# Sparse attention: where the bias tile is loaded, how the mask is made, and the order of the splits and fills

## The chip, the cores and the metric

One core of one Trainium2 chip runs the whole program in one launch. TensorE multiplies matrices; VectorE, ScalarE and GpSimd work on tiles in on-chip memory (SBUF, and PSUM for matmul results); SyncE, and here also ScalarE and GpSimd, issue the DMAs. The metric is the device time of one execution in microseconds, as the median of several executions. The profile is one further execution, recorded by the hardware profiler.

## The reference, cut to what matters

A two-layer model with 256 tokens of 1024 features: a recurrent layer with an MLP, a sparse attention layer with an MLP, and a closing block. The change concerns the sparse attention: an indexer scores all keys of a query, the 64 best causal keys are kept, and softmax runs over these with a bias that depends on the distance and the head.

```python
q, c, qi, ki, wi = jnp.split(h @ w_in, ATT_IN_SPLITS, axis=-1)
...
dots = jax.nn.relu(jnp.einsum('bqhd,bsd->bqhs', qi_b, ki))          # 8 index heads
score = jnp.einsum('bqh,bqhs->bqs', wi_b, dots)
score = jnp.where(causal[None], score, -jnp.inf)
_, idx = lax.top_k(score, topk)                                     # topk = 64
...
bias = jnp.moveaxis(rel_bias[t5_bucket(dist)], -1, 2)               # by distance, 16 heads
logits = jnp.einsum('bqhc,bqkc->bqhk', q_lat_b, c_sel) + bias
logits = jnp.where((dist >= 0)[:, :, None, :], logits, -jnp.inf)
p = jax.nn.softmax(logits, axis=-1)
return jnp.einsum('bqhk,bqkc->bqhc', p, c_sel)
```

The kernel doesn't gather. It computes the logits of all keys and adds a very large negative number (NEG, -1e30) to those that are not among the 64 or lie in the future.

## The kernel before, in words

**Products.** Every float32 product is made of three matmuls of a faster 32-bit type, on the high and the low part of both operands (mm3, L235 to L239). Each weight chunk of 128 x 1024 numbers (512 KB) therefore takes three steps (wt_part, L222 to L225): SyncE's queue loads it into w_raw, ScalarE copies it to w_hi, and VectorE subtracts and gets w_lo. There are four buffers for w_raw and six each for w_hi and w_lo. While K.pool is set, GpSimd does the subtraction instead (pooled), and that split is put behind the last score instruction issued so far (K.scored).

**Order.** Most instructions go to a tile scheduler, which orders them for each engine by priorities. Where K.pin is set, or keep_in_program_order is called, the instruction stands in the order of the source. An order written out by hand interleaves the parts of the attention: run(s0, n) advances the scores of query block 0 by n steps, and pooled(next_q), q_half(i), k_part(j) and v_part(h) are put between. After it, a list of fills gives TensorE something to do between a turn and the product that follows it.

**Stages.** rec_layer; mlp(0), in 16 groups, each with an up and a down product, into which hook0 mixes other work: ada_raw loads on SyncE's queue with dot products on VectorE, and, in group 2, t5_bias_rows, which computes 16 rows (one per head) of 384 bias numbers by distance and writes them to DRAM by GpSimd's queue (t5_rows); att_layer; mlp(1); the closing block.

**The attention.** cki is the projection that holds the latent, the index key and the head weights. qi_ps are the four index-query projections (two pairs), from chunks 2 to 5 of w_att_in. tz is a tile of 128 x 16 x 256 numbers: for each query row and head the bias row, shifted by one number from row to row. It is read from t5_rows in four DMAs of 512 KB with rows of 1 KB; they stand on ScalarE's queue behind the low part of the last weight chunk (load_tz, L704 to L712). scores(t) makes the score of query block t: eight heads on TensorE, ScalarE and VectorE, and then eight rounds of MAX and MATCH_REPLACE on VectorE, each of which finds the eight largest numbers and replaces them by TAKEN. The mask follows (L833 to L840): dg is the larger of "not taken" and noncausal on the diagonal 128 x 128 square, and msk is dg times NEG; block 1 also has a first square without a diagonal. q_half(0..7) are the query projections (two make one q_ps and one qT); k_part makes the keys and v_part the values. soft adds bias and mask (l_mb, L877), makes the logits (l_ps, L886), adds both with a running maximum (l_s, L893; l_nm is its negative), and ScalarE takes exponentials (L899). turn transposes the result (pT_ps, copied to pT by VectorE or ScalarE in turn, L915 and L917), weigh multiplies by the values (o_ps, L927), and o_sb divides by the sum.

Of the kernel before, what the change touches and what calls it, by code (L numbers as in the profile page):

```python
# [10 lines left out]
F32 = mybir.dt.float32  # L11
# [3 lines left out]
ALU = mybir.AluOpType  # L15
# [5 lines left out]
P = 128  # L21
S = 256
# [11 lines left out]
NEG = -1e30  # L34
LOWEST = -3e38
TAKEN = -3.4e38
TAKEN_CUT = -3.2e38
IDX_W_SCALE = 8 ** -0.5 * 64 ** -0.5
NBKT, MAXD = 32, 128
TZW = 384  # L40
# [119 lines left out]
def _tile_stack(ctx, tc, ins, out):  # L160
    nc = tc.nc
    K = _Ctx()
# [3 lines left out]
    pin = tc.keep_in_program_order  # L166
    const = ctx.enter_context(tc.tile_pool(name="const", bufs=1))
# [7 lines left out]
    def behind(later, earlier):  # L175
        tc.add_manual_dep(later.ins, earlier.ins.name,
                          mybir.DependencyInfo(mybir.DependencyClass.Sync, mybir.DependencyReason.DATA),
                          reason="load order")
# [51 lines left out]
    def wt(src, k):  # L230
        raw, hi, lo = wt_tiles()
        wt_part(raw, hi, lo, src, slice(0, CH))
        return [h.rearrange("p (k c) -> p k c", k=k) for h in (hi, lo)]
# [443 lines left out]
    def att_layer():  # L677
        with tc.tile_pool(name="att", bufs=1) as a1, tc.tile_pool(name="att2", bufs=2) as a2:
            att_body(a1, a2)

    def att_body(a1, a2):
# [15 lines left out]

        xT = transposed(xt, "mix1", (0, 1), lambda: c.append(wt(ins["w_att_in"][1], 4)), cki_rows, cki_rows)
        wq = [wt(ins["w_att_in"][2 + i], KT) for i in range(2)]
        K.pin = False  # L700
        rs = [rms_stat(xt[t], "r") for t in range(2)]
        b = cki[0]
        tz_after = wt.last
        tz = a1.tile([P, 16, S], F32, name="tz")  # L704

        def load_tz(after):
            for q in range(4):
                behind(nc.scalar.dma_start(tz[:, 4 * q:4 * q + 4],
                                           bass.AP(tensor=K.t5_rows.tensor, offset=K.t5_rows.offset + 1 + 4 * q * TZW,
                                                   ap=[[1, P], [TZW, 4], [1, S]])), after)  # L710

        load_tz(tz_after)  # L712

        noncausal = K.noncausal
        low = a1.tile([P, S], F32, name="low")
        nc.vector.memset(low[:, :P], 0.0)
# [65 lines left out]
        def k_part(j):  # L782
            b = ps("k_ps")
            for i in range(2):
                col = (2 * j + i) * P
                mm3(b[:, i * S:(i + 1) * S], [h[:, 0, col:col + P] for h in uk], (cTh, cTl), True, True)
            k = a1.tile([P, 2, S], F32, name=f"kT{j}")
            nc.scalar.activation(k.rearrange("p a b -> p (a b)"), b, AF.Copy)
            kT.extend([k[:, 0], k[:, 1]])
# [15 lines left out]
        def scores(t):  # L805
            nk = P * (t + 1)
            sc = [a1.tile([P, nk], F32, name=f"score{t}_{i}") for i in range(2)]
            prev = low[:, S - nk:]
            hb = 512 // nk
            parts = []  # L810
            for g in range(8 // hb):
                b = ps("sc_ps")
                par, base = g % 2, (g // 2) * 2 * hb
                hl = [base + par + 2 * j for j in range(hb)]
                o = par * 64
                for j, h in enumerate(hl):
                    nc.tensor.matmul(b[:, j * nk:(j + 1) * nk], qiT[h // 2][o:o + 64, t * P:(t + 1) * P],
                                     kiT[o:o + 64, :nk], start=True, stop=True)
                r = a2.tile([P, 512], F32, name="sc_r")
                rl = nc.scalar.activation(r, b, AF.Relu)  # L820
                for j, h in enumerate(hl):
                    m = pin(nc.vector.scalar_tensor_tensor(sc[0], r[:, j * nk:(j + 1) * nk], wis[t][:, h:h + 1], prev,
                                                       op0=ALU.mult, op1=ALU.add))
                    prev = sc[0]
                    K.scored = m
                yield
            for rd in range(8):
                mx = a2.tile([P, 8], F32, name="top8")
                pin(nc.vector.max(out=mx, in_=sc[rd % 2]))
                pin(nc.vector.match_replace(out=sc[(rd + 1) % 2], in_to_replace=mx, in_values=sc[rd % 2],  # L830
                                            imm_value=TAKEN))
                yield
            m = a1.tile([P, nk], F32, name=f"msk{t}")  # L833
            if t:
                pin(nc.vector.tensor_scalar(m[:, :P], sc[0][:, :P], TAKEN_CUT, NEG, op0=ALU.is_gt, op1=ALU.mult))
            dg = a2.tile([P, P], F32, name="dg")
            pin(nc.vector.scalar_tensor_tensor(dg, sc[0][:, nk - P:], TAKEN_CUT, noncausal,
                                               op0=ALU.is_gt, op1=ALU.max))
            pin(nc.vector.tensor_scalar(m[:, nk - P:], dg, NEG, None, op0=ALU.mult))
            msk.append(m)  # L840

        qT = []
# [1 line left out]
        def q_half(i):  # L844
            if i == len(qw):
                next_q()
            if i % 2 == 0:
                q_half.b = ps("q_ps", "acc")
            b = q_half.b
            j = i % 2  # L850
            prod_a(b[:, j * S:(j + 1) * S], qw[i], xT)
            if j:
                q = a1.tile([P, 2, S], F32, name=f"qT{i // 2}")
                m = nc.vector.scalar_tensor_tensor(q, b.rearrange("p (j s) -> p j s", j=2), 0.125, rB2,
                                                   op0=ALU.mult, op1=ALU.mult)
                if K.pin:
                    pin(m)
                qT.extend([q[:, 0], q[:, 1]])
# [114 lines left out]
        def run(steps, n=1):  # L973
            for _ in range(n):
                next(steps, None)
# [7 lines left out]
        def soft_pair(m):  # L983
            gr, it = items[m]
            return [(gr, it + i, *sh) for i, sh in enumerate(soft(gr, it))]

        def pooled(f):
            K.pool = True
            f()
            behind(wt.last, K.scored)  # L990
            K.pool = False

        uv = []
        s0, s1 = scores(0), scores(1)
        run(s0, 2)
        next_q()
        run(s1, 2)
        q_half(0)
        run(s1, 2)
        q_half(1)  # L1000
        pooled(lambda: uv.extend(wt(ins["w_att_ukv"][1], 1)))
        run(s0, 5)
        pooled(next_q)
        q_half(2)
        run(s0, 4)
        v_part(0)
        q_half(3)
        pooled(next_q)
        pend = soft_pair(0)
        run(s1, 4)  # L1010
        k_part(2)
        q_half(4)
        pooled(next_q)
        run(s1, 5)
        K.pin = False
        fills = [units(), units((q_half, 5)), units((k_part, 3)), units((q_half, 6)), units((q_half, 7)),
                 units((v_part, 1)), units()]
# [3 lines left out]
        for m in range(6):  # L1021
# [7 lines left out]
            pend = cur  # L1029
# [7 lines left out]
    def t5_bias_rows(const):  # L1037
        rb = const.tile([NBKT, 16], F32, name="rel_bias")
        nc.gpsimd.dma_start(rb, ins["rel_bias"])
        oh = const.tile([NBKT, TZW], F32, name="onehot")  # L1040
        nc.gpsimd.dma_start(oh, ins["onehot"])
        b = ps("t5_ps")
        nc.tensor.matmul(b[:16, :TZW], rb, oh, start=True, stop=True)
        r = const.tile([16, TZW], F32, name="t5_sb")
        nc.vector.tensor_copy(r, b[:16, :TZW])
        rows = dram.tile([16, TZW], F32, name="t5_rows")
        nc.gpsimd.dma_start(rows, r)
        return rows
# [4 lines left out]
    def ada_start():  # L1053
        cond = vec("cond", 0, 16)
        th = sm.tile([P, 16], F32, name="silu_t", bufs=1)
        behind(nc.scalar.activation(th, cond, AF.Tanh, scale=0.5), wt.last)
        nc.vector.scalar_tensor_tensor(th, th, 1.0, cond, op0=ALU.add, op1=ALU.mult)
        nc.vector.tensor_scalar(th, th, 0.5, None, op0=ALU.mult)
        ada.update(sc=th, ad=const.tile([P, 16, 2], F32, name="ada"))
# [546 lines left out]
                nc.sync.dma_start(out[0, t * P:(t + 1) * P, sl], f)  # L1606

    rec_layer()
    with tc.tile_pool(name="mlp0", bufs=2) as mp:
        ada_start()  # L1610

        def hook0(g):
            if g == 0:
                K.steps = ada_steps(mp)
            if g == 2:
                K.t5_rows = t5_bias_rows(mp)
                K.noncausal = const.tile([P, P], F32, name="noncausal")
                behind(nc.gpsimd.dma_start(K.noncausal, ins["noncausal"]), K.last)
            next(K.steps, None)
            if g in (7, 12):  # L1620
                next(K.steps, None)
        mlp(0, lambda name, dt: mp.tile([P, 2 * S], dt, name=name), hook0)
    att_layer()
    with tc.tile_pool(name="blk", bufs=1) as b1, tc.tile_pool(name="blk2", bufs=2) as b2:
        early = []

# [32 lines left out]
```

## Time and profile before

| what | value |
|---|---|
| time, median of 3 runs | 896.39 us (893.65 to 897.42) |
| profiled execution | 895.19 us, its span 893.4 us |
| TensorE matmuls (PE) | 876.2 us busy, 98%, 5502 instructions |
| VectorE (DVE) | 684.7 us, 77%, 1191 |
| ScalarE (ACT) | 464.2 us, 52%, 744 |
| GpSimd (POOL) | 51.4 us, 6%, 62 |
| DMA | 162.81 MB, 182 GB/s in the mean |

The span is the time from the first recorded instruction to the last. A share of the span is a mean over stages: the attention is a small part of it, from about 270 to 390 us, and its gaps are seen on the timeline of the engine that sets the end, not in the table. A timeline row has a start and a duration; rows of TensorE overlap, since matmuls are pipelined, so the pitch from start to start counts and not the duration. In brackets stands the idle time before the row and the instruction whose end released it. Names ending in q (ACTq, SPq) are the engine's DMA issues.

### The profile page before, as it was taken

What the parts mean: (1) busy time and instruction counts of PE and PEld (TensorE: products, weight loads), DVE (VectorE), ACT (ScalarE), POOL (GpSimd) and SP (SyncE); (2) the same over time, 40 slices, a digit from 0 to 9 for tenths busy, and PEclk for the clock granted to TensorE, in tenths of its full rate; (3) what the DMA queues carried; (4) which work ended last, traced back from release to release, by engine and by line L of the source; (5) the groups of instructions that cost most, each with busy time, mean ns of one, the idle gap of its engine ahead of it and who ended that gap; (6) DMA issues with size and microseconds to landing.
All of it is one profiled execution on the core that took longest, in us unless ns stands there. A gap on an engine that the chain in (4) does not pass through costs nothing.

```text
span 893.4 us, 14243 instructions
## 1 busy us (share of the span) xinstructions
PE 876.2 (98%) x5502; PEld 777.8 (87%) x5502; DVE 684.7 (77%) x1191; ACT 464.2 (52%) x744; POOL 51.4 (6%) x62
## 2 busy tenths in 40 slices
PE   9999999999999989999999999999999999999998
PEld 7998888888888877888788888898899999989997
DVE  6979789999665898587687777777779987557665
ACT  6895654444455556465465444464445444445441
POOL 3400100000001120000000000111010000000000
PEclk9999999999999999999999999999999999999999
DMA  6646678886653631327976666345253444434541
GB/s 260 209 147 209 230 244 289 285 285 216 212 188 94 213 129 61 143 91 254 289 234 221 231 253 221 118 163 168 95 187 101 162 142 139 145 118 165 182 150 48
DMA packets 47575, 162.81 MB, mean 182 GB/s; under 512 B 5217, under 2 KB 8561, under 8 KB 47506
## 3 DMA queue, kind: packets, MB, share of 16 engines
q1 hardware_dynamic: 44690, 158.39, 52.2%
q10 hardware_dynamic: 2400, 2.31, 0.9%
q0 software_dynamic: 416, 1.19, 0.4%
q8 instruction: 43, 0.70, 0.3%
q14 instruction: 26, 0.21, 0.1%
HBM read 160.80 MB, written 1.07 MB: 181 GB/s over the span
## 4 chain that ended last, share of the span: by engine, by line
PE 71%; issue 17%; DVE 6%; DMA 3%; ACT 1%; POOL 1%; ACTq 0%; SPq 0%; POOLq 0%; DVEq 0%
PE up_ps L249 12%; PE acc_ps L239 7%; PE acc_ps L237 7%; PE acc_ps L238 7%; PE up_ps L252 6%; PE acc_ps L280 2%; PE z_ps L239 2%; PE z_ps L238 2%; PE z_ps L237 2%; PE pj_ps L239 2%; PE pj_ps L237 2%; PE pj_ps L238 2%; DVE w_lo L225 1%; DMA nb<-in_rpb_dram 1%; PE mg_ps L239 1%
## 5 line engine op out<-in xcount | busy, mean ns | idle before, releaser
L224 ACT ACTIVATE w_hi<-w_raw 128x1024 fp32r<-128x1024 f32 (+1 forms) x269 | 278.0, 1054 | 210.2 <-PE z_ps L238 63.8
L225 DVE TENSOR_TENSOR w_lo<-w_raw,w_hi 128x1024 fp32r<-128x1024 f32 (+1 forms) x265 | 318.0, 1215 | 86.7 <-ACT w_hi L224 86.2
L249 PE MATMUL up_ps<-xT,w_hi 128*128 128x512 f32 x480 | 170.7, 398 | 0.0
L252 PE MATMUL up_ps<-xT,w_lo 128*128 128x256 f32 x480 | 134.8, 281 | 0.0
L237 PE MATMUL z_ps<-h,w_hi 128*128 128x256 f32 x416 | 119.0, 286 | 0.0
L238 PE MATMUL z_ps<-h,w_hi 128*128 128x256 f32 x416 | 118.4, 285 | 0.0
L239 PE MATMUL z_ps<-h,w_lo 128*128 128x256 f32 x416 | 117.8, 283 | 0.0
L249 PEld LDWEIGHTS up_ps<-xT,w_hi 128*128 128x128 f32 x480 | 90.2, 188 | 21.9
L237 PE MATMUL acc_ps<-w_hi,mlp_hi 128*128 128x512 f32 x240 | 94.2, 392 | 0.0
L238 PE MATMUL acc_ps<-w_lo,mlp_hi 128*128 128x512 f32 x240 | 93.7, 390 | 0.0
L239 PE MATMUL acc_ps<-w_hi,mlp_lo 128*128 128x512 f32 x240 | 93.4, 389 | 0.0
L252 PEld LDWEIGHTS up_ps<-xT,w_lo 128*128 128x128 f32 x480 | 90.7, 189 | 1.1
L237 PEld LDWEIGHTS z_ps<-h,w_hi 128*128 128x128 f32 x416 | 79.7, 192 | 0.4 <-issue 0.3
L238 PEld LDWEIGHTS z_ps<-h,w_hi 128*128 128x128 f32 x416 | 79.7, 192 | 0.1
L239 PEld LDWEIGHTS z_ps<-h,w_lo 128*128 128x128 f32 x416 | 79.7, 192 | 0.1
L301 ACT ACTIVATE mlp_hi<-mlp_h 128x512 fp32r<-128x512 f32 (+1 forms) x34 | 20.6, 606 | 88.8 <-DVE mlp_h L655 84.2
L1351 DVE SCALAR_TENSOR_TENSOR cc_a<-cc_u,half_ccw,cc_a 128x256 f32<-128x256 f32 x120 | 56.3, 481 | 2.3 <-ACT na_s L1432 0.5
L237 PEld LDWEIGHTS acc_ps<-w_hi,mlp_hi 128*128 128x128 f32 x240 | 45.1, 188 | 10.6 <-ACT w_hi L224 0.6
L239 PEld LDWEIGHTS acc_ps<-w_hi,mlp_lo 128*128 128x128 f32 x240 | 45.1, 188 | 9.8 <-DVE mlp_lo L302 0.2
L238 PEld LDWEIGHTS acc_ps<-w_lo,mlp_hi 128*128 128x128 f32 x240 | 45.1, 188 | 8.3
L1078 DVE CUSTOM_DVE_ANT_0 ada_t<-ada_raw,ada_c 128x1024 f32<-128x1024 f32 x32 | 38.6, 1207 | 0.0
L302 DVE TENSOR_TENSOR mlp_lo<-mlp_h,mlp_hi 128x512 fp32r<-128x512 f32 (+1 forms) x34 | 22.2, 654 | 9.8 <-ACT mlp_hi L301 9.8
(384 smaller groups left out, 1684.4 us busy)
## 6 DMA issues: line engine op xcount, KB each, us to landing
w_raw<-in_w_up_dram SPq DMA_DIRECT2D x64, 512.0 KB, 4.5
w_raw<-in_w_down_dram SPq DMA_DIRECT2D x64, 512.0 KB, 4.4
w_raw<-in_w_gate_dram SPq DMA_DIRECT2D x24, 512.0 KB, 3.5
ada_raw<-in_w_adaT_dram SPq DMA_DIRECT2D x16, 512.0 KB, 4.6
w_raw<-in_w_qkvz_dram SPq DMA_DIRECT2D x16, 512.0 KB, 3.5
w_raw<-in_w_bb_dram SPq DMA_DIRECT2D x16, 512.0 KB, 3.5
w_raw<-in_w_rec_in_dram SPq DMA_DIRECT2D x15, 512.0 KB, 4.7
w_raw<-in_w_att_in_dram SPq DMA_DIRECT2D x14, 512.0 KB, 4.3
```

The costliest lines, as they stand in the source:

```text
L224: a = nc.scalar.activation(hi[:, sl], raw[:, sl], AF.Copy)
L225: wt.last = (nc.gpsimd if K.pool else nc.vector).tensor_sub(lo[:, sl], raw[:, sl], hi[:, sl].bitcast(F32))
L237: nc.tensor.matmul(o, wh, xh, start=first, stop=False)
L238: nc.tensor.matmul(o, wh, xl, start=False, stop=False)
L239: nc.tensor.matmul(o, wl, xh, start=False, stop=last)
L249: nc.tensor.matmul(b, wh, bass.AP(tensor=hi.tensor, offset=hi.offset, ap=[hi.ap[0], [lo.offset - hi.offset, 2], hi.ap[-1]]), start=k == 0, ...
L252: nc.tensor.matmul(b[:, :S], wl, hi, start=False, stop=k == KT - 1)
L280: nc.tensor.matmul(acc[t][h], c[i][1][xi][:, t * P:(t + 1) * P], c[i][0][wi][:, 0, h * 512:(h + 1) * 512], start=False, stop=xi == 1 and i ...
L301: nc.scalar.activation(hi, src, AF.Copy)
L302: nc.vector.tensor_sub(lo, src, hi.bitcast(F32))
L1078: nc.vector.tensor_tensor_reduce(out=th, in0=raw, in1=rows[n], op0=ALU.mult, op1=ALU.add, scale=1.0, scalar=0.0, accum_out=dot[:, j, n:n + 1])
L1351: t = nc.vector.scalar_tensor_tensor(a, u[:, k:k + S], hw[:, 4 * k + j:4 * k + j + 1], a, op0=ALU.mult, op1=ALU.add)
```

## The change

The bias tile tz moves from the attention's pool to a pool of its own, opened ahead of mlp(0), and its four DMAs are issued by SyncE, in the source behind the loads of the first two index-query chunks; the scheduler places them. The bias rows carry the causal mask: the 128 numbers for future keys are NEG, and only the other 256 are copied. The mask is then one instruction, on the whole block, and dg is gone. In the order by hand GpSimd takes five splits instead of four, the one for q_half(3) ahead of the one for the values; k_part(2) stands ahead of q_half(3); v_part(0) stands behind the first soft.

```diff
+        tz = K.tz
+        for q in range(4):
+            nc.sync.dma_start(tz[:, 4 * q:4 * q + 4],
+                              bass.AP(tensor=K.t5_rows.tensor, offset=K.t5_rows.offset + 1 + 4 * q * TZW,
+                                      ap=[[1, P], [TZW, 4], [1, S]]))
         K.pin = False
...
-        tz_after = wt.last
-        tz = a1.tile([P, 16, S], F32, name="tz")
...
-        load_tz(tz_after)
-
...
             m = a1.tile([P, nk], F32, name=f"msk{t}")
-            if t:
-                pin(nc.vector.tensor_scalar(m[:, :P], sc[0][:, :P], TAKEN_CUT, NEG, op0=ALU.is_gt, op1=ALU.mult))
-            dg = a2.tile([P, P], F32, name="dg")
-            pin(nc.vector.scalar_tensor_tensor(dg, sc[0][:, nk - P:], TAKEN_CUT, noncausal,
-                                               op0=ALU.is_gt, op1=ALU.max))
-            pin(nc.vector.tensor_scalar(m[:, nk - P:], dg, NEG, None, op0=ALU.mult))
+            pin(nc.vector.tensor_scalar(m, sc[0], TAKEN_CUT, NEG, op0=ALU.is_gt, op1=ALU.mult))
...
         q_half(1)
+        pooled(next_q)
+        run(s0, 5)
         pooled(lambda: uv.extend(wt(ins["w_att_ukv"][1], 1)))
-        run(s0, 5)
+        q_half(2)
+        run(s0, 3)
+        k_part(2)
         pooled(next_q)
-        q_half(2)
-        run(s0, 4)
+        q_half(3)
+        run(s0)
+        pend = soft_pair(0)
         v_part(0)
-        q_half(3)
+        run(s1, 4)
         pooled(next_q)
-        pend = soft_pair(0)
-        run(s1, 4)
-        k_part(2)
         q_half(4)
+        run(s1, 2)
         pooled(next_q)
-        run(s1, 5)
+        run(s1, 3)
...
-        nc.vector.tensor_copy(r, b[:16, :TZW])
+        nc.vector.memset(r[:, :P], NEG)
+        nc.vector.tensor_copy(r[:, P:], b[:16, P:TZW])
...
+    with tc.tile_pool(name="keep", bufs=1) as kp:
+        K.tz = kp.tile([P, 16, S], F32, name="tz")
```

SyncE's queue in the middle of the first MLP, before: w_raw are weight chunks, ada_raw the side work of hook0.

```order
L223 DMA w_raw<-in_w_down_dram 128x1024 x2
L1075 DMA ada_raw<-in_w_adaT_dram 128x1024
L223 DMA w_raw<-in_w_up_dram 128x1024 x2
L1075 DMA ada_raw<-in_w_adaT_dram 128x1024
L223 DMA w_raw<-in_w_down_dram 128x1024 x2
```

The same place after, where tz is the bias tile and t_rows the bias rows in DRAM:

```order
L223 DMA w_raw<-in_w_down_dram 128x1024 x2
L702 DMA tz<-t_rows 128x4x256
L1068 DMA ada_raw<-in_w_adaT_dram 128x1024
L223 DMA w_raw<-in_w_up_dram 128x1024 x2
L1068 DMA ada_raw<-in_w_adaT_dram 128x1024
L223 DMA w_raw<-in_w_down_dram 128x1024 x2
L1068 DMA ada_raw<-in_w_adaT_dram 128x1024
L702 DMA tz<-t_rows 128x4x256
```

The first two of the four bias loads stand here, the first directly ahead of an ada_raw load and both ahead of a pair of up weights; the third and the fourth follow later, each between an ada_raw load and a pair of up weights, behind the eighth and the tenth ada_raw load of the program.

VectorE at the end of block 0's rounds, before (top and score are the rounds' tiles; msk, l_mb, l_s, l_mx and qT as in the description above):

```order
L829 MAX top_3389<-score_1_3221 128x8
L830 MATCH_REPLACE score_0_3220<-top_3389,score_1_3221 128x128
L837 SCALAR_TENSOR_TENSOR dg<-score_0_3220,noncausal 128x128
L839 TENSOR_SCALAR msk_3392<-dg 128x128
L877 TENSOR_TENSOR l_mb<-tz,msk_3392 128x512 x2
L854 SCALAR_TENSOR_TENSOR qT_3430<-q_ps,rB 128x512
L893 ISA l_s,l_mx<-l_ps,l_mb 128x128
```

The same place after:

```order
L823 MAX top_3393<-score_1_3225 128x8
L824 MATCH_REPLACE score_0_3224<-top_3393,score_1_3225 128x128
L843 SCALAR_TENSOR_TENSOR qT_3435<-q_ps,rB 128x512
L828 TENSOR_SCALAR msk_3437<-score_0_3224 128x128
L866 TENSOR_TENSOR l_mb<-tz,msk_3437 128x512 x2
L882 ISA l_s,l_mx<-l_ps,l_mb 128x128
```

dg is gone, and qT has moved from behind the mask and the bias sums to the place right behind the last round.

TensorE from the logits to the first product with the values, before (kT and qT are keys and queries, xT the transposed input, v the values):

```order
L886 MATMUL l_ps<-kT_3201,qT_3329 128x256 x4
L193 MATMUL pT_ps<-ident,l_s 128x128 x4
L237 MATMUL q_ps<-xT_2841,w_hi 128x256
L238 MATMUL q_ps<-xT_2841,w_hi 128x256
L239 MATMUL q_ps<-xT_2841,w_lo 128x256
L237 MATMUL q_ps<-xT_2841,w_hi 128x256
L238 MATMUL q_ps<-xT_2841,w_hi 128x256
L239 MATMUL q_ps<-xT_2841,w_lo 128x256
L237 MATMUL q_ps<-xT_2842,w_hi 128x256
L238 MATMUL q_ps<-xT_2842,w_hi 128x256
L927 MATMUL o_ps<-v_3192,pT 128x64 x4
```

The same place after:

```order
L875 MATMUL l_ps<-kT_3205,qT_3333 128x256 x4
L193 MATMUL pT_ps<-ident,l_s 128x128 x4
L916 MATMUL o_ps<-v_3196,pT 128x64 x4
L193 MATMUL pT_ps<-ident,l_s 128x128 x4
L237 MATMUL q_ps<-xT_2846,w_hi 128x256
L238 MATMUL q_ps<-xT_2846,w_hi 128x256
```

The eight q_ps matmuls that stood between the first pT_ps and o_ps have moved behind o_ps and the second pT_ps.

## Rows read from the trace of the kernel before

**Rows 1.** Busy by stretch: us, engines' busy (count), granted clock, DMA share, GB/s.

```profile
120.00:165.00 45.00, 45.00 (x228) 38.05 (x228) 45.00 (x66) 22.48 (x33) 1.06 (x2) 1.00 0.81 267
292.00:297.00 5.00, 5.00 (x44) 5.00 (x44) 3.21 (x5) 1.70 (x3) 0.00 (x0) 1.00 1.08 387
320.00:325.00 5.00, 4.93 (x31) 4.81 (x32) 4.03 (x26) 2.76 (x3) 1.15 (x1) 0.66 0.07 28
```

**Rows 2.** TensorE's timeline: start, us, work [idle before, what ended it].

```profile
288.99 0.28 PE L239 MATMUL qi_ps<-xT,w_lo 128*128 128x256 f32 x1
...
291.61 0.39 PE L239 MATMUL qi_ps<-xT,w_lo 128*128 128x256 f32 x1 [1.52 <-DVE w_lo L225]
...
311.66 0.40 PE L237 MATMUL v_ps<-w_hi,cTh 128*128 128x512 f32 x1
...
313.47 0.28 PE L237 MATMUL q_ps<-xT,w_hi 128*128 128x256 f32 x1
313.59 0.28 PE L238 MATMUL q_ps<-xT,w_hi 128*128 128x256 f32 x1
314.52 0.39 PE L239 MATMUL q_ps<-xT,w_lo 128*128 128x256 f32 x1 [0.66 <-POOL w_lo L225]
...
320.07 0.72 PE L886 MATMUL l_ps<-kT,qT 64*128 64x128 f32 x8 [2.01 <-DVE qT L854]
...
325.99 1.13 PE L886 MATMUL l_ps<-kT,qT 64*128 64x256 f32 x8
...
340.75 0.28 PE L239 MATMUL q_ps<-xT,w_lo 128*128 128x256 f32 x1
342.55 0.44 PE L193 MATMUL pT_ps<-ident,l_s 128*128 128x128 f32 x2 [1.52 <-ACT l_s L899]
```

**Rows 3.** ScalarE's timeline, 280 to 300 us.

```profile
284.62 3.02 ACTq L708 DMA_DIRECT2D tz<-t_rows  x4
287.74 0.31 ACT L307 ACTIVATE sq<-cki 128x128 f32<-128x128 f32 x1 [4.68 <-issue]
```

**Rows 4.** VectorE's timeline at cki.

```profile
284.84 0.75 DVE L725 TENSOR_SCALAR cki<-cki_ps,rstd 128x200 f32<-128x200 f32 x2
```

**Rows 5.** SyncE's queue, first MLP.

```profile
129.24 0.33 SPq L1075 DMA_DIRECT2D ada_raw<-in_w_adaT_dram  x1
```

**Rows 6.** DMA in 284 to 296 us: a queue's share, one group of issues.

```profile
q10 hardware_dynamic: 2103, 2.09, 57.0%
...
tz<-t_rows ACTq DMA_DIRECT2D x4, 512.0 KB, 7.9
```

**Rows 7.** VectorE's timeline, 309 to 340 us.

```profile
315.74 2.09 DVE L837 SCALAR_TENSOR_TENSOR dg<-score,noncausal 128x128 f32<-128x128 f32 x1
...
318.12 1.29 DVE L877 TENSOR_TENSOR l_mb<-tz,msk 128x512 f32<-128x512 f32 x2
...
320.82 0.29 DVE L893 CUSTOM_DVE_ANT_0 l_s<-l_ps,l_mb 128x128 f32<-128x128 f32 x1 [0.80 <-PE l_ps L886]
...
326.71 0.43 DVE L829 MAX8 top<-score 128x8 f32<-128x256 f32 x1
327.75 0.69 DVE L917 COPY pT<-pT_ps 128x512 f32<-128x512 f32 x1 [0.61 <-PE pT_ps L193]
...
335.91 0.28 DVE L837 SCALAR_TENSOR_TENSOR dg<-score,noncausal 128x128 f32<-128x128 f32 x1
...
339.74 0.16 DVE L897 TENSOR_SCALAR l_nm<-l_mx 128x2 f32<-128x2 f32 x1
```

**Rows 8.** GpSimd's timeline, 300 to 332 us.

```profile
309.72 4.75 POOL L225 TENSOR_TENSOR w_lo<-w_raw,w_hi 128x1024 fp32r<-128x1024 f32 x2 [19.63 <-DVE score L822]
315.29 2.40 POOL L225 TENSOR_TENSOR w_lo<-w_raw,w_hi 128x1024 fp32r<-128x1024 f32 x1 [0.82 <-ACT w_hi L224]
```

**Rows 9.** ScalarE's timeline, 320 to 331 us.

```profile
323.79 1.28 ACT L899 ACT_TABLE_LOAD   x1
...
328.18 1.99 ACT L224 ACTIVATE w_hi<-w_raw 128x1024 fp32r<-128x1024 f32 x2
```

More of the change, by code (lines that the diff above doesn't have):

```diff
@@ L702, in att_body @@
         b = cki[0]
-        tz_after = wt.last
-        tz = a1.tile([P, 16, S], F32, name="tz")
[L706 to L710, printed above, removed]
-        load_tz(tz_after)
         noncausal = K.noncausal
@@ L1608, in _tile_stack, with hook0 @@
     rec_layer()
[L1609 to L1620, printed above, removed]
+    with tc.tile_pool(name="keep", bufs=1) as kp:
+        K.tz = kp.tile([P, 16, S], F32, name="tz")
+        with tc.tile_pool(name="mlp0", bufs=2) as mp:
+            ada_start()
+            def hook0(g):
+                if g == 0:
+                    K.steps = ada_steps(mp)
+                if g == 2:
+                    K.t5_rows = t5_bias_rows(mp)
+                    K.noncausal = const.tile([P, P], F32, name="noncausal")
+                    behind(nc.gpsimd.dma_start(K.noncausal, ins["noncausal"]), K.last)
                 next(K.steps, None)
-        mlp(0, lambda name, dt: mp.tile([P, 2 * S], dt, name=name), hook0)
-    att_layer()
+                if g in (7, 12):
+                    next(K.steps, None)
+            mlp(0, lambda name, dt: mp.tile([P, 2 * S], dt, name=name), hook0)
+        att_layer()
     with tc.tile_pool(name="blk", bufs=1) as b1, tc.tile_pool(name="blk2", bufs=2) as b2:
```

## The prediction

> **What bounds the kernel now.** Read first the table by stretch [rows 1]: in 120 to 165 us, inside the first MLP, TensorE is busy 45.00 of 45.00 us, so nothing done there can make the kernel faster, only slower. Then the sparse attention (about 270 to 390 us) on TensorE's own timeline, where the gaps stand [rows 2]. The pitch of the projection's 256-column matmuls is 0.12 us (313.47 to 313.59). Four gaps are larger than that:
> - qi_ps: the third matmul after the one at 288.99 was due at 289.35 and starts at 291.61: 2.26 us lost, ended by VectorE's w_lo.
> - q_ps: due at 313.71, starts at 314.52: 0.81 us, ended by GpSimd's w_lo.
> - l_ps: 2.01 us before 320.07, ended by VectorE's qT.
> - pT_ps: due at 340.87, starts at 342.55: 1.68 us, ended by ScalarE's exponentials.
>
> They make 6.8 us. Behind the third one the granted clock is 0.66 of 2.4 GHz in 320 to 325 [rows 1]: part of that stretch ran at 1.2 GHz, and 0.34 x 5 = 1.7 us of full speed are missing. 8.5 us is therefore all that the change can win, under 1% of the time.
>
> **The change part by part.**
>
> *The bias load leaves ScalarE.* Its four issues occupy ScalarE from 284.62 to 287.64; the small squares of cki wait behind them until 287.74 although VectorE has written cki at 284.84 + 0.4 = 285.25 [rows 3, 4]. The squares, the reciprocal root, cn and the splits follow each other, so all move by 287.74 - 285.25 = 2.49 us: the split that TensorE got at 291.61 is there at 289.12, before it is wanted at 289.35. The gap goes: -2.26 us. What would be late next are the weights themselves, but both were loaded long before. Bounds: nothing (if a weight is late) to -2.26; I take -2.26. Scores, top-8 rounds and everything behind shift with it.
>
> *The load itself goes to SyncE's queue in the first MLP.* The order shows it not late there but spread over its middle, one issue beside the fourth, the sixth, the eighth and the tenth load of ada_raw; those positions come up from 129.24 on [rows 5]. In the attention the four transfers took 57.0% of 12 us of all 16 engines, 6.84 us, or 1.7 us each [rows 6]. In the MLP the engines are busy 0.81 of 45 us [rows 1], which leaves 8.6 us. So 0; if none of that free time were usable, at most 6.84 us slower. The attention's own queue is emptier than before. The first issue waits for the bias rows to be written; the next instruction on the queue only goes at 129.24 anyway. The memset in the rows' tile and the shorter copy lie in the same full stretch: 0.
>
> *The mask.* Block 0 replaces dg and msk by one instruction. dg there took 2.09 us, while its twin in block 1 takes 0.28 [rows 7]; the difference is 1.81, and it ends 0.14 us after GpSimd's split (315.29 to 317.69) does [rows 8]. So dg was held by the split. The Trainium skill (SBUF — State Buffer, Who interferes with whom) states this: a VectorE instruction with two SBUF inputs and a GpSimd one that reads SBUF exclude each other for the whole instruction; this trace agrees with 2.09 against 0.28. By that rule the hold does not end with dg: l_mb (tz and msk, both in SBUF) and VectorE's own splits are as exposed.
>
> *The order.* GpSimd now splits q_half(3)'s weights first and the v weights second, starting when the last score is done: 309.72 - 2.26 = 307.46, with 2.40 us each [rows 8]: 309.86, 312.26, and 314.66 for q_half(4)'s. TensorE did v_part at 311.66 and then q_half(3); now six k_ps matmuls stand in that place, so q_half(3) starts at 311.66 - 2.26 + 6 x 0.12 = 310.1 and finds its weights: -0.81. Its 24 matmuls end at 313.1, four l_ps after it at 313.8. VectorE ends its rounds at 315.74 - 2.26 = 313.48 and now does qT first: l_ps goes on at about 314.25 after 0.45 us instead of 2.01: -1.55. Then msk and l_mb: free at 314.1, but held to 314.66 if the split excludes them; l_mb takes 1.3 us, so l_s starts at 315.55 or 316.15, against 320.82 before [rows 7]. VectorE is 4.7 to 5.3 us earlier.
>
> TensorE is earlier still. From 314.25 it does the eight l_ps (0.72), six v_ps of twice the columns (6 x 0.24), q_half(4) (24 x 0.12) and the next l_ps (1.13 before [rows 2]), so the first pT_ps starts at 320.4 (before: 325.99 + 1.13 = 327.1), and its four are done at 320.85. There the order takes away its cover: o_ps now follows pT_ps directly, where eight q_ps matmuls stood between. o_ps needs VectorE's copy of pT, and this stands behind l_s and four and a half top-8 rounds of block 1: from 320.82 to 326.71 + 0.42 before, 6.31 us [rows 7]. That is 321.85 or 322.45; with the reciprocal and the copy's 0.69, 322.7 or 323.3. So a **new wait of 1.9 to 2.5 us**; I take 2.3, nearer to the held end, since dg's row shows a hold. ScalarE's table load and eight exponentials (323.79 to 328.18 before, 4.39 us) [rows 9] then end near 321.5 and are not last.
>
> Block 1: three mask instructions become one, one split moves to GpSimd, and the order has two of VectorE's four splits less between the copy of pT and l_nm. That stretch took 339.74 - 327.75 = 11.99 us [rows 7]; begun at 322.6 it ends at 334.6 even in full, and with one or two exponentials of about half a us the turn is fed at 335.1 to 335.6. The two splits fewer are set against a hold: VectorE's next one may wait for GpSimd's last, at most 2.40 us. TensorE had 340.87 - 327.1 = 13.75 us from the first pT_ps to this one; the order has 11 q_ps fewer in it (1.3 us) and the new wait, so it arrives at 320.4 + 13.75 - 1.3 + 2.3 = 335.15. Both come together: the fourth gap goes, -1.68, with 0.2 as the small end if the hold is full and only one split's worth (1.2 us) is given back.
>
> *The clock.* Before, it fell behind idles of 0.81 and 2.01 us; behind the 2.26 us at 289 to 291.6 it stayed at 1.00 [rows 1]. The new idle is of that same size, so the rows allow either. I take it as falling again, at 0, since 0.45 and 2.3 resemble the pair before which it fell; the other end is -1.7.
>
> Sum: -2.26 - 0.81 - 1.55 - 1.68 + 2.3 = **-4.0 us**. The profiled execution took 895.19 us (span 893.4 and 1.8 around it), so 891.2; the median shown is 896.39, 1.2 above that, so **892.4 us** is forecast. The rest of the program is TensorE-bound with the same instructions, so the gain should be kept to the end. Ends of the terms: -0.8 - 1.5 - 0.2 + 2.5 = 0, and -6.3 + 1.9 - 1.7 = -6.1; with the runs' own spread of 3.8 us (893.65 to 897.42) that gives 888 to 896.5.
>
> **The rivals.**
> 1. *The clock stays up and nothing is held.* -6.1 us: 890.3. For it: the clock was 1.00 after the first gap. Against: dg's 2.09.
> 2. *The gain is handed back on VectorE.* GpSimd has five splits instead of four. If l_mb is held through one more of them, 2.40 us, the wait before o_ps is 4.7 and block 1 is as late: 4.0 - 2.4 and some 1.0 at the fourth gap, -0.6 us: 895.8. For it: the same hold as dg's. Against: q_half(5)'s split needs a w_hi that now stands behind the v copies on ScalarE, so GpSimd should be idle when l_mb starts.
> 3. *SyncE's queue starves the first MLP: slower.* An issue there stands ahead of weights, and its 1 KB rows may be served slowly. The loads landed 7.9 us after issue in the crowded attention [rows 6]. If each held the weights behind it that long, 31.6 us, less 8.6 of free engine time, would be 23.0: with -4.0, 915.4. It decides once a load holds the queue for more than (8.6 + 4.0) / 4 = 3.15 us. Against: 1.7 us of engine time each, and in the attention weights and bias shared the engines.
> 4. *It does not do what it says:* the load is not late in the MLP. As worked out above this costs nothing by itself.
>
> **How the numbers follow.** Forecast (-2.5 to -5.5): 0.55, its own range 890.5 to 894. Rival 1: 0.17. Rival 2 (0 to -2.5): 0.20. Rival 3: 0.08. A change under 0.5%, 4.5 us, can't be told from none here. Faster by more: half of the forecast and rival 1, 0.44. Within: the other half and nearly all of rival 2, 0.47. Slower: 0.09. The range of 888 to 896.5 leaves out rival 3 and the outer parts of 1 and 2.
>
> **What would show it.** Right: four tz issues on SyncE between 128 and 165 us with TensorE busy throughout; no gap over 0.3 us at the third qi_ps chunk; GpSimd's first three splits back to back and no wait on them in q_half(3); qT ahead of msk; an idle of 2 us between the first pT_ps and o_ps, ended by VectorE's copy; no wait for exponentials before block 1's pT_ps. Wrong: any TensorE gap in the first MLP, l_mb over 0.8 us, or a second wait of over 1 us in block 1.

## The result, and the profile after

The changed kernel takes 887.61 us in the median (885.75 to 888.95, 4 executions) against 895.31 for the kernel before: ratio 0.9917, interval 0.9899 to 0.9935. A second set of executions gave 887.70 and 0.9918 (0.9901 to 0.9936). That is 6.8 to 7.7 us faster; 4.0 had been forecast, and 887.61 lies just outside the stated range of 888 to 896.5. (The forecast of 892.4 was counted from 896.39, the median of three runs before; with a fourth it is 895.31, so 1.1 of the 4.8 us between forecast and result is the base, and 3.7 are the gain.) The profiled execution took 887.87 us, its span 886.1 (before 893.4).

Busy time by stretch, as in [rows 1] (the middle stretch lies where the first gap was):

```profile
120.00:165.00 45.00, 45.00 (x227) 38.04 (x227) 45.00 (x66) 21.48 (x30) 1.06 (x2) 1.00 0.87 298
289.00:294.00 5.00, 5.00 (x45) 5.00 (x43) 3.61 (x5) 1.39 (x4) 0.00 (x0) 1.00 0.62 202
320.00:325.00 5.00, 3.02 (x24) 2.22 (x22) 4.72 (x16) 4.89 (x14) 2.12 (x1) 1.00 0.00 0
```

The first MLP is full as before, with the DMA engines at 0.87 instead of 0.81. The granted clock is 1.00 in 320 to 325, where it was 0.66; that is this one execution, and the second profile of the same kernel (after_again, below) shows a fall. SyncE's queue issues the bias loads where the order had them, first and last here:

```profile
129.84 0.39 SPq L702 DMA_DIRECT2D tz<-t_rows  x1
...
162.50 0.43 SPq L702 DMA_DIRECT2D tz<-t_rows  x1
```

TensorE's timeline at the places of [rows 2]:

```profile
314.41 0.72 PE L875 MATMUL l_ps<-kT,qT 64*128 64x128 f32 x8 [0.34 <-DVE qT L843]
```

```profile
320.58 0.66 PE L193 MATMUL pT_ps<-ident,l_s 128*128 128x128 f32 x4
323.21 1.10 PE L916 MATMUL o_ps<-v,pT 128*128 128x64 f32 x8 [1.98 <-DVE pT L906]
...
325.30 0.38 PE L239 MATMUL q_ps<-xT,w_lo 128*128 128x256 f32 x1 [0.30 <-POOL w_lo L225]
```

```profile
332.00 1.13 PE L875 MATMUL l_ps<-kT,qT 64*128 64x256 f32 x4 [0.30 <-DVE o_sb L925]
...
336.32 0.44 PE L193 MATMUL pT_ps<-ident,l_s 128*128 128x128 f32 x2
```

The 2.01 us before l_ps are 0.34 now; the first pT_ps starts at 320.58 (forecast 320.4) and o_ps at 323.21 (forecast 322.7 to 323.3), behind the forecast new wait: 1.98 us idle, ended by VectorE's copy of pT. Block 1's pT_ps, which lost 1.68 us to the exponentials, now starts only 0.17 us later than the usual pitch. Two waits of 0.30 us are new. VectorE and GpSimd, to set beside [rows 7, 8]:

```profile
313.68 0.68 DVE L843 SCALAR_TENSOR_TENSOR qT<-q_ps,rB 128x512 f32<-128x512 f32 x1
314.27 0.68 DVE L828 TENSOR_SCALAR msk<-score 128x128 f32<-128x128 f32 x1
...
325.44 3.25 DVE L225 TENSOR_TENSOR w_lo<-w_raw,w_hi 128x1024 fp32r<-128x1024 f32 x1
```

```profile
307.76 7.10 POOL L225 TENSOR_TENSOR w_lo<-w_raw,w_hi 128x1024 fp32r<-128x1024 f32 x3 [19.70 <-DVE score L816]
322.88 4.73 POOL L225 TENSOR_TENSOR w_lo<-w_raw,w_hi 128x1024 fp32r<-128x1024 f32 x2 [8.01 <-ACT w_hi L224]
```

GpSimd's splits end at 307.76 + 7.10 = 314.86 and at 327.61. The mask, one instruction with one input, takes 0.68 us and ends at 314.95; block 1's, on twice the columns and beside no split, takes 0.28. VectorE's split at 325.44 takes 3.25 us instead of 1.21 and ends 1.1 us, about its own length, after GpSimd's.

From the first qi_ps matmul to the first up_ps of the second MLP TensorE took 108.02 us before and 99.93 after, 8.09 less. (Ahead of that stretch the execution after is 0.37 us later, and behind it 0.4 us more is lost, so the spans differ by 7.3. Executions of one kernel differ by as much there: in the second profile of the changed kernel the stretch begins 0.75 us earlier than in this one.) From start to start of the matmuls, against their usual pitch, the 8.09 us are:

| place | forecast, us | measured, us |
|---|---|---|
| gap at the third qi_ps chunk | -2.26 | -2.33 |
| gap in q_half(3) | -0.81 | -0.92 |
| gap before l_ps | -1.55 | -1.68 |
| new wait before o_ps | +2.3 | +2.15 |
| gap before block 1's pT_ps | -1.68 | -1.5 |
| clock (18 or so matmuls at 0.21 instead of 0.12) | 0 | -1.6 |
| wait in v_part(0) for the split | not seen | -0.3 |
| two waits of 0.30 us idle | not seen | +0.9 |
| three waits before o_ps, 344 to 358 | not seen | -1.2 |
| logits that stand together, 340 to 364 | not seen | -1.3 |
| other changes of order behind block 1's pT_ps | not seen | -0.3 |

The last three rows make 2.8 us, all behind block 1's first pT_ps. The three waits stood in the timeline of the kernel before:

```profile
344.61 1.10 PE L927 MATMUL o_ps<-v,pT 128*128 128x64 f32 x8 [0.25 <-ACT kT L788]
...
350.67 1.10 PE L927 MATMUL o_ps<-v,pT 128*128 128x64 f32 x8 [0.31 <-DVE pT L917]
...
357.56 0.66 PE L927 MATMUL o_ps<-v,pT 128*128 128x64 f32 x4 [0.34 <-DVE pT L917]
```

and the last group of logits was in two pieces there, 0.86 us and 1.09 us to the next start (359.79 to 360.65, 362.63 to 363.72), where it now takes 1.09 in one (354.92 to 356.01):

```profile
359.79 0.93 PE L886 MATMUL l_ps<-kT,qT 64*128 64x128 f32 x6
...
362.63 1.16 PE L886 MATMUL l_ps<-kT,qT 64*128 64x128 f32 x10
363.72 0.55 PE L193 MATMUL pT_ps<-ident,l_s 128*128 128x128 f32 x3
```

```profile
354.92 1.16 PE L875 MATMUL l_ps<-kT,qT 64*128 64x128 f32 x16
356.01 0.66 PE L193 MATMUL pT_ps<-ident,l_s 128*128 128x128 f32 x4
```

That is 0.86 us of the 1.3. The other 0.4 are eight logits of 256 columns, which stood in two groups of four (1.06 and 1.05 us to the next start) and now stand in six and two (1.06 and 0.63).

### The profile page after: what moved, and what is told of

Same layout as the page of the kernel before. It is cut to its first block, busy times and chain, and to the rows that moved or that the text cites. A ratio compares the mean times of both kernels' runs of the same rounds, so it can differ in the third digit from the quotient of the medians.

```text
span 886.1 us, 14240 instructions
## 1 busy us (share of the span) xinstructions
PE 871.5 (98%) x5502; PEld 774.9 (87%) x5502; DVE 683.6 (77%) x1188; ACT 464.0 (52%) x744; POOL 53.7 (6%) x63
## 4 chain that ended last, share of the span: by engine, by line
PE 71%; issue 18%; DVE 6%; DMA 3%; ACT 1%; POOL 1%; SPq 0%; POOLq 0%; DVEq 0%; ACTq 0%
PE up_ps L249 12%; PE acc_ps L237 7%; PE acc_ps L238 7%; PE acc_ps L239 7%; PE up_ps L252 6%; PE acc_ps L280 2%; PE z_ps L239 2%; PE z_ps L238 2%; PE z_ps L237 2%; PE pj_ps L239 2%; PE pj_ps L237 2%; PE pj_ps L238 2%; DMA nb<-in_rpb_dram 1%; PE mg_ps L239 1%; PE mg_ps L238 1%
```

## The experiments

All were timed beside the kernel before; ratios are to it, and "the changed kernel" has 887.7 (0.9918). The runs stand on several chips, on which the kernel before has medians from 893.9 to 895.4, so that ratios compare better than times. The mean granted clock of whole executions is given as the result of each lists it.

**a_tz_only.** Only the load.

```diff
-        load_tz(tz_after)
+        tz = K.tz                 # own pool, four nc.sync.dma_start behind wq
```

> The kernel before, with the bias tile in its own pool and its four loads on SyncE's queue; mask and order as before. Theory (the terms add up): only the gap of 2.3 us at the third qi_ps chunk goes, so 895.3 - 2.3 = 893.0; the gaps of 0.81 (q_ps) and 2.29 (l_ps) stay, and the granted clock falls behind the second as before (0.66 in some 5 us), so the gap at 289 us has no part in that. Rival (the bias load pays more than its wait): the load's place in the attention's queue also held the weights behind it, so 4 us or more go. Rival (handed back): VectorE and GpSimd come no earlier and the 2.3 us stand in a later gap, 895.

Measured: 892.88, ratio 0.9978 (0.9966 to 0.9989). The stretch of the attention is 2.32 us shorter, the gaps in q_half(3) and before l_ps are there (0.68 and 1.99 us idle), and the clock falls behind the second:

```profile
315.00:320.00 5.00, 3.01 (x23) 2.60 (x20) 3.76 (x19) 0.00 (x0) 0.00 (x0) 0.76 0.30 105
```

The first term stands, and the clock falls without the first gap: it does in the profile, and the mean of all 11 executions is 0.998 or less.

**b_mask_only.** Only the bias rows with NEG and the one-instruction mask.

```diff
-            pin(nc.vector.scalar_tensor_tensor(dg, sc[0][:, nk - P:], TAKEN_CUT, noncausal, ...
-            pin(nc.vector.tensor_scalar(m[:, nk - P:], dg, NEG, None, op0=ALU.mult))
+            pin(nc.vector.tensor_scalar(m, sc[0], TAKEN_CUT, NEG, op0=ALU.is_gt, op1=ALU.mult))
```

> The kernel before, with NEG in the bias rows and the mask in one instruction; load and order as before. Theory (the mask's one instruction is held by GpSimd's split just as dg was): it ends where dg ended, and only the 0.23 us of the second instruction go, here and in block 1: 895.1, l_ps gap 2.0 to 2.1 us instead of 2.29. Rival (the hold belongs to two-input instructions alone): the mask takes 0.28 us, the gap shrinks by 1.9 us and the clock stays at 1.00, 892 or less.

Measured: 891.93, ratio 0.9962 (0.9947 to 0.9977). The mask was held just as dg was:

```profile
314.66 2.00 DVE L834 TENSOR_SCALAR msk<-score 128x128 f32<-128x128 f32 x1
```

so the rival is out, and the gap before l_ps lost only 0.36 us. Yet the kernel is 2.7 us faster, which neither theory had: from oT_ps (343.76 before, 341.61 here) to the pT_ps behind the last logits (363.72, 359.31) it takes 17.70 us instead of 19.96. The scheduler's order there is another one: the last logits stand together, the eight ahead of them in six and two, and of the three waits of 344 to 358 the second is gone and the third down to 0.16 us. In this profile the clock also stayed at 1.00, behind idle times of 0.69 and 1.66 us.

**c_order_only.** Only the order of splits and fills.

> The kernel before, with the new order of GpSimd's splits and of the fills alone; load and three-instruction mask as before. Theory (the order carries most of it): the gaps of 0.81, 0.30 (v_ps) and 1.7 of 2.29 us go, and with them the fall of the clock (1.7 us): -4.5; further down the wait for the exponentials (1.7) shrinks and logits stand in pairs again (1.0): 889 in all, -5.5 to -7. Between the first pT_ps and o_ps nine q_ps stand here, so the wait of 2.25 us of the changed kernel is not here. Rival (the parts need each other: without the earlier start VectorE is as late as before): -3 or less, 892 or more, with a gap of over 1 us left at l_ps.

Measured: 892.41, ratio 0.9965 (0.9953 to 0.9977): the rival's size, but not with its gap. The gap before l_ps is down to 0.34 idle. The rest is lost in a wait of 2.98 us before o_ps, and behind it the clock falls (0.67 in 325 to 330). VectorE, GpSimd and TensorE:

```profile
319.84 2.37 DVE L897 TENSOR_SCALAR l_nm<-l_mx 128x4 f32<-128x4 f32 x1
```

```profile
319.81 2.37 POOL L225 TENSOR_TENSOR w_lo<-w_raw,w_hi 128x1024 fp32r<-128x1024 f32 x1 [3.50 <-ACT w_hi L224]
```

```profile
327.12 0.69 PE L927 MATMUL o_ps<-v,pT 128*128 128x64 f32 x2 [2.98 <-DVE pT L917]
```

l_nm, 128 x 4 numbers with one input, began 0.03 us after GpSimd's split and lasted as long as it. Everything behind it on VectorE, the rounds and the copy of pT, was late by 2.2 us.

**d_order_q5_dve.** As c, with that split on VectorE.

```diff
-        pooled(next_q)
+        next_q()
         q_half(4)
```

> The kernel before with the new order alone, but the split for q_half(5) on VectorE instead of GpSimd. Theory (in the order-only kernel l_nm, 128 x 4 numbers, took 2.37 us because GpSimd's split began at the same moment; VectorE's rounds, the copy of pT and o_ps were late by that much): l_nm takes 0.17 us; a split of 1.2 us stands ahead of the copy of pT instead, so the wait before o_ps shrinks from 3.26 to 1.5 to 2.3 us; 891.3 against 892.4, and the clock falls in fewer executions. Rival (the wait before o_ps is due to the number of rounds ahead of the copy, not to l_nm): 3 us or more stay, and 1.2 are added, 893.5.

Measured: 890.94, ratio 0.9966 (0.9952 to 0.9981). l_nm takes 0.17 us and the wait before o_ps is gone; q_half(5) waits 1.70 us for its split on VectorE instead. So l_nm was the cause of that wait in c. In time nothing was won that the runs can tell: the ratio is that of c (0.9965), since the other wait came in its place. The clock did not fall less often: 1.0 in 1 of 10 executions.

**u_unpair.** Loops over the heads' halves exchanged in soft.

```diff
-            for j in range(hb):
-                for par in range(2):
+            for par in range(2):
+                for j in range(hb):
```

> The changed kernel, but the logits of one half of the heads are all made before those of the other (loop order in soft), so that no matmul on rows 0 to 63 is followed by one on rows 64 to 127. Theory (two such matmuls run at the same time): of 32 logits with 128 columns, 16 pairs at 0.105 us become 32 at 0.11, +1.9 us; of 32 with 256 columns 16 pairs at 0.21 become 32 at 0.21, +3.4; some stand ahead of a wait that takes them up, so +3.5 to +5 on 887.6: 891 to 892.6. Rival (they do not overlap on the array; the 0.007 us between the two are a matter of the record): no change, 887.6.

Measured: 888.11, ratio 0.9923 (0.9907 to 0.994): no difference that can be told from 887.7. The edit hardly did what it was to do: in the trace, matmuls of the two halves still start 0.013 us apart wherever a group has four of each. Why they do is not shown. Only the last group, eight logits of one half ahead of eight of the other, is longer, 1.64 us instead of 1.09:

```profile
354.57 1.71 PE L875 MATMUL l_ps<-kT,qT 64*128 64x128 f32 x16
356.21 0.55 PE L193 MATMUL pT_ps<-ident,l_s 128*128 128x128 f32 x3
```

So the time of the whole run can't decide between the two theories, but this group does: the same sixteen matmuls take half as long again where the halves are parted. The two halves do run beside each other, and the price is 0.5 us for the one group, not the 3.5 to 5 us expected.

**v1_v.** v_part(1) as the first fill of the changed kernel.

```diff
-        fills = [units(), units((q_half, 5)), ..., units((v_part, 1)), units()]
+        fills = [units((v_part, 1)), units((q_half, 5)), ..., units(), units()]
```

> The changed kernel with v_part(1) as the first fill instead of the sixth, so that six v_ps (1.4 us) and some q_ps stand between the first pT_ps and o_ps. Theory (the new wait of 2.25 us there is lost cover, and VectorE's copy comes when it did): the wait shrinks below 0.7 us, -1.5 to -2; at the old place of v_part(1) some 0.5 us come back: 886 to 886.5 against 887.6. If idle time is what brings the clock down, its fall becomes rarer too (mean granted clock 0.999 or more in most executions). Rival (TensorE's work is only moved, and the end is set by VectorE's chain of rounds, mask and l_s of block 1): the 2 us stand again in a wait ahead of block 1's pT_ps at 336, 887.6.

Measured: 886.67, ratio 0.9923 (0.9911 to 0.9935): the same as the changed kernel. The wait is moved, not filled:

```profile
322.29 0.50 PE L237 MATMUL v_ps<-w_hi,cTh 128*128 128x512 f32 x1 [1.29 <-DVE pT L906]
...
324.38 0.39 PE L239 MATMUL q_ps<-xT,w_lo 128*128 128x256 f32 x1 [0.76 <-POOL w_lo L225]
```

The second v_ps is released by the very copy of pT, and q_half(5) waits for GpSimd's split. Neither theory had that: the fill itself was not ready.

**v4_dve, v5_v_dve.** GpSimd's last split on VectorE, alone and with v1_v's fill (edit as in d, at the last pooled(next_q)).

> The changed kernel with GpSimd's last split given back to VectorE (four splits on GpSimd, as before). Theory (VectorE's split of 3.25 us at 325.44 is held by GpSimd's pair until 327.6, and only 1.2 of it is work): it takes 1.2 us, VectorE does one more split of 1.2 us and is still 0.8 us earlier at block 1's mask; the wait of 0.46 us for o_sb goes; -0.3 to -0.8: 887. Rival (the 3.25 us are something else, such as the chunk's w_hi being late): the split still takes over 2 us and VectorE is 1.2 us later, +0.5 or more.

> Both of these at once. Theory: the two add up, 885.5 (-1.5 to -2.5 against 887.6). Rival (VectorE's chain sets block 1): only the better of the two is kept.

Measured: 887.80, ratio 0.9937 (0.9921 to 0.9953), and 887.77, 0.9933 (0.9919 to 0.9947): no gain from either. VectorE's split takes 1.86 us instead of 3.25, since the one GpSimd split beside it ends earlier (at 323.94), but VectorE has one more to do:

```profile
323.16 1.86 DVE L225 TENSOR_TENSOR w_lo<-w_raw,w_hi 128x1024 fp32r<-128x1024 f32 x1
```

**after_again, v7, v7b.** The changed kernel again, and two versions in which q_half(5)'s weights are early: ScalarE's part ahead of the v copies, GpSimd's split behind l_nm, beside the rounds. In v7 q_half(5) is also the first fill.

```diff
+        early = hi_part()          # load and ScalarE's copy, ahead of q_half(3)
         q_half(3)
         run(s0)
         pend = soft_pair(0)
+        lo_part(*early)            # GpSimd's split, behind(m, K.nm), the last l_nm
-        fills = [units(), units((q_half, 5)), ...
+        fills = [units((q_half, 5)), units(), ...
```

> The changed kernel once more, unchanged, for a comparison on one chip with the two below and for more executions with their mean granted clock: 887.6, the ratio to before 0.9917 to 0.993; executions at 1.0 about 886.3, those at 0.998 or less 887.5 to 889.5.

> The changed kernel with q_half(5) as the first fill, so that 24 q_ps (2.9 us) stand between the first pT_ps and o_ps; its weights are made ready for that: ScalarE's high part is moved ahead of the v copies, and GpSimd's split is put behind l_nm, so that it lies beside VectorE's rounds MAX and MATCH_REPLACE, which no split has held so far. Theory (the wait of 2.25 us is lost cover, and v1_v failed only because these weights were late): no gap over 0.7 us from the logits to block 1's pT_ps; VectorE's split that took 3.25 us takes under 2; -2 to -2.7 against the changed kernel: 885. If idle time brings the clock down, most executions have 0.999 or 1.0. Rival (block 1 is set by VectorE's chain): the 2 us come back as a wait ahead of block 1's pT_ps; 887.

> As v7, but with q_half(5) as the second fill, as in the changed kernel: the weights alone are made ready early. The order has eight q_ps (1.0 us) between the first pT_ps and o_ps. Theory: the wait shrinks from 2.25 to 1.3 us and the wait of 0.46 us for GpSimd's split goes; 886.2. Rival: as above, 887.5.

Measured: 887.70; v7 884.63, ratio 0.9888 (0.9867 to 0.9909); v7b 885.34, 0.9896 (0.9877 to 0.9916). In the profile of after_again the wait before o_ps is the same, and behind it the clock fell (0.74, where the first profile of this kernel has 1.00):

```profile
322.48 1.10 PE L916 MATMUL o_ps<-v,pT 128*128 128x64 f32 x8 [2.01 <-DVE pT L906]
```

```profile
325.00:330.00 5.00, 5.00 (x32) 4.90 (x32) 5.00 (x6) 1.67 (x2) 1.83 (x1) 0.74 0.69 223
```

v7 is 3.1 us faster than the changed kernel on the same chip, the fastest of all here, and the rival is out. About half of the 3.1 us is the clock: the changed kernel's two executions at 1.0 on that chip took 886.3 in the mean, v7's four 884.8. v7b, with the early weights alone, has 2.4 of the 3.1; the rest, the fill's place, can't be told from nothing. GpSimd's split, VectorE's and the product in v7:

```profile
317.28 2.38 POOL L983 TENSOR_TENSOR w_lo<-w_raw,w_hi 128x1024 fp32r<-128x1024 f32 x1 [3.61 <-DVE l_nm L886]
```

```profile
323.26 1.89 DVE L225 TENSOR_TENSOR w_lo<-w_raw,w_hi 128x1024 fp32r<-128x1024 f32 x1
```

```profile
322.73 1.00 PE L916 MATMUL o_ps<-v,pT 128*128 128x64 f32 x8
```

Beside the split VectorE's rounds keep their pitch of 0.98 us for a round, the split on VectorE takes 1.89 us instead of 3.25, and o_ps starts with no idle time. All four executions have a granted clock of 0.999.

**w_long.** More idle time: eight additional MAX on VectorE.

```diff
+                if t and rd == 2:
+                    for _ in range(8):
+                        extra = a2.tile([P, 8], F32, name="extra")
+                        pin(nc.vector.max(out=extra, in_=sc[(rd + 1) % 2]))
```

> The changed kernel with eight additional MAX instructions (their results go unused) behind the third round of block 1 on VectorE, five of them ahead of the copy of pT. They take 8 x 0.44 = 3.5 us of VectorE; the copy stands one and a half rounds earlier, so the wait before o_ps grows by 5 x 0.44 - 1.5 = 0.7 to 0.9 us to some 3.1, and the rest comes as a wait ahead of block 1's pT_ps. Theory (idle time of TensorE brings the clock down): +3.5 us for the waits and 1 to 1.7 more for the clock, mean granted clock 0.997 or less in most executions: 892 to 893. Rival (the clock falls by chance, whatever TensorE does): the clock is spread as in the changed kernel (1.0 in 4 of 10, mean 0.998): 887.7 + 3.5 = 891.2. Rival (VectorE has slack there): 888.

Measured: 890.52, ratio 0.9965 (0.9939 to 0.9991), between the theories. The wait did not grow: 1.62 us idle now end at two q_ps that stand ahead of o_ps, and o_ps starts 0.3 us late behind them. The rest, 1.52 us idle, came before block 1's pT_ps. The clock falls in 320 to 330:

```profile
320.00:325.00 5.00, 3.25 (x20) 2.69 (x20) 4.97 (x15) 4.08 (x10) 2.87 (x2) 0.86 0.00 0
325.00:330.00 5.00, 5.00 (x33) 4.88 (x33) 4.53 (x7) 2.48 (x3) 2.90 (x1) 0.80 0.51 157
```

In 11 of 12 executions the mean granted clock is 0.997 or less (three have 0.988 to 0.990 and take 896.3 to 899.5 us), against 4 of 10 for the changed kernel.

## Why the prediction was wrong

**The step that failed is the sum, where it says that "the rest of the program is TensorE-bound with the same instructions, so the gain should be kept to the end".** The working ended at block 1's first pT_ps, and so did the count ahead of it, four gaps and the clock, 8.5 us as "all that the change can win". Behind 342.55 the change won 2.8 us more, 2.5 of them in 344 to 364: three waits before o_ps, and logits in pieces. Both are rows of the trace and of the order of before. The experiments show what they go with. From block 1's first pT_ps to the pT_ps behind the last logits it takes 21.2 us before and in a, 18.9 in b, 19.8 in c and in d (with one acc_ps, 0.2, more), and 19.7 in the changed kernel, of which 1.3 are eleven q_ps that stood ahead of it before. So the load has no part in it; the mask alone and the order by hand alone each bring part of it, 2.3 and 1.6, and the two do not add up.

Against this stand 0.9 us that the prediction did not have, two small waits behind the split and o_sb. At equal clock the account closes: executions at 1.0 take 893.1 us before and 886.6 after, 6.6 less, which is the 4.0 forecast and 2.6 more.

**The clock's term was taken at 0 and was -1.6 between the two profiles compared.** The reason given, that 0.45 and 2.3 us resemble the pair before which it fell, does not hold as a rule: behind the same wait of 2.0 us idle the clock stayed at 1.00 in one profile of the changed kernel and fell in the other. It is a chance in each execution. Before, the mean granted clock was 1.0 in 8 of 62 executions, after in 4 of 10. So in the medians the clock is worth less than between these two profiles. The Trainium skill (TensorE: Matmul & The Clock Gate, Part 1) says that what the gate watches runs freely and is not tied to the kernel's start, so that one kernel varies from run to run; the 62 executions agree.

Rival 1 (890.3) came nearest in time, but by luck: the clock stayed up in some executions only, the mask and a split were held, and its -6.1 us has nothing of the 2.8. Right, and near the size forecast: the load (a), the gaps in q_half(3), before l_ps and before block 1's pT_ps, and the new wait with its place, its cause and its 2.15 us. (340.87 - 327.1 is 13.77 and not 13.75; nothing hangs on it.) The load in the MLP cost nothing, so rival 3 fell (TensorE 45.00 of 45.00). Rival 2's mechanism is real and struck in c, at l_nm instead of l_mb; in the changed kernel it did not, for the reason given there: GpSimd's fourth split came late, at 322.88, when l_nm was done. What it took instead was 2.0 us of VectorE's split at 325.44 (at most 2.40 had been allowed for it), mostly off TensorE's path.

The prediction held dg and l_mb to be exposed because both their inputs lie in SBUF. That was too narrow: the mask (2.00 us in b) and l_nm (2.37 in c) have one input. The Trainium skill (SBUF — State Buffer, Who interferes with whom) adds that tensor_scalar can enter a mode that takes both ports and then contends too; these two rows agree. MAX and MATCH_REPLACE were not held beside a split in any trace here.

Open: why the scheduler's order at 344 to 364 depends on the mask instructions and on the order ahead of it; nothing tried here separates its reasons. That idle time raises the chance of the clock's fall is borne out by the runs together, on several chips: a mean clock of 0.998 or less stands in 3 of 19 executions of v1_v, v5_v_dve, v7 and v7b, which parted, shortened or filled the wait before o_ps, in 16 of 22 of the changed kernel, u_unpair and v4_dve, which have it whole, and in 11 of 12 of w_long. Why one execution falls and the next does not stays open.

## What to carry to other kernels

Carry a sum of waits to the end of the stage that the scheduler orders anew: set the two orders side by side down to the last moved instruction, and price the waits that stand there before, not only those that the change names. Before a fill is moved into a wait, ask what the fill itself waits for: here it was the same copy and the same split, and the gain came only when its weights were made ready first. Put GpSimd's splits beside VectorE's MAX and MATCH_REPLACE, not beside its small one-input instructions on SBUF. Before a profile's clock is put into a sum, take a second profile of the same kernel.

## What the hardware showed that was not expected

An instruction on 128 x 4 numbers took 2.37 us instead of 0.17, because a GpSimd split had begun 0.03 us before it. Logits on rows 0 to 63 and on rows 64 to 127 of the array start 0.007 us apart and run side by side; the way into and out of such a group costs some 0.1 us each (0.20 us from start to start instead of 0.11). The Trainium skill (TensorEngine Tiling (Array Packing), Key Properties) has both: such tiles are independent of each other, and a change of the mode drains the array. The starts here agree.
